# Conv accumulators in pairs, six input blocks ahead of the first gate, weight stores in ScalarE's queue: a hybrid S5/Conformer layer

## Chip, cores and metric

One core of a Trainium2 chip. The metric is the device time of one execution in microseconds: the median of three runs.

## What is computed

One decoder layer over a prompt of 2048 rows of width 1024, and beside it one step for each of 8 decoding sequences. All data is float32.

```python
h = rmsnorm(x); p = h @ w_in                      # 1024 -> 512 (S5 input u) + 512 (conv value) + 512 (conv gate)
s = s5(u)                                         # 32 groups, 64 complex states: h_t = A h_(t-1) + B u_t
a = gelu(Re(C h) + D u); s = a * sigmoid(a @ w_glu + b_glu)
z = value * sigmoid(gate)
c = swish(layernorm(causal_dwconv31(z)))          # 31 taps for each channel
x = x + rmsnorm(concat(s, c) @ w_out)
u = causal_dwconv3(rmsnorm(x) @ w_up)             # 1024 -> 2 x 2816
y = x + rmsnorm((silu(u_gate) * u_val) @ w_down)  # 2816 -> 1024
```

The last states and the last rows of both convolutions are outputs too.

## The kernel before

**Tiles and rounds.** The positions are cut into six tiles, five of 344 and one of 328 with the 8 decoding rows behind it (TILES, L24). Two tiles make a round. Activations lie with channels on partitions. Each matrix product is done with three float32r products: weights and activations are split into a high part (rounded, by ScalarE) and a low part (the rest, by VectorE), and `group` (L1105) issues high x high, high x low and low x high for each slice of 128 rows. A group of a w_in block is 24 matmuls for one tile, so a block is 48 for a round.

**Order of TensorE's work.** ORDER (L32) lists it: the input projection of rounds 0 and 1 (`mix_in`, L1954), four of the twelve blocks of round 2, then the gate and output projection of round 0 (`mix_out`, L2008, "out(0)" below), the other eight blocks, then the ConvFFN (`ffn`, L2071) of round 0, and so on. IN_ORDER (L31) gives the blocks' order: 0 to 3 make u, 4 to 7 the conv value, 8 to 11 the conv gate. `mix_out` starts with the product with w_glu, the first gate, then takes eight w_out blocks for each tile: their first four slices read sHL (the gated S5 output), their last four cHL (the split conv output).

**Weights.** `w_next` (L872) hands out blocks in the order of the list `wl`. A block's first use loads it raw (`w_load_to`, L835), splits it (`w_split_to`, L851: ScalarE writes wh, VectorE wlo) and, if it is used again, stores both parts in device memory (wd, L865 to L867). Later uses load the two parts. Each of wraw, wh and wlo has three buffers. All these transfers are issued by SyncE (SP).

**Work beside it.** Generators run beside the main order: the S5 parts (`s5_part`: products into R, a scan on VectorE in place, products into ya), the depthwise convolution (`conv`, L1677), the norms (`mid`, L1799: residual, second norm; `split_ffn`, L1813: splits its output into h for the ConvFFN). `spawn` gives each a due time; `tick` lets them emit while an estimate of each engine's clock stays within a lead of TensorE's. `after(ns)` makes a generator wait; the norms wait by NORM (L42). What is recorded so is put into the final order of each engine by a list scheduler (`Recorder.place`, L253), which works with estimated durations; on the chip each engine runs its own list in order.

**The conv.** For each of four channel blocks k and each half of a round (344 or 336 positions), 31 VectorE instructions accumulate the taps into a PSUM tile of the pool ps_cv (one bank): the first multiplies and adds the bias, the others multiply by a tap's weight and add the accumulator, the last writes the result to SBUF over the input. In round 0, block 0 and the second half of block 1 are done by ScalarE and GpSimd (`conv_pool`, L1653).

**PSUM.** Eight banks: four for matrix products (ps_mm), one for the conv (ps_cv), three for transposes and small products (ps_tr), the last counted by TRP (L682).

Of the kernel before, what the change touches and what calls it, by code (L numbers as in the profile page):

```python
# [7 lines left out]
F32 = mybir.dt.float32  # L8
# [10 lines left out]
KC = 31  # L19
# [9 lines left out]
S5_TURN = [7500, 7500, 7500]  # L29
PARTS = [4, 4, 4, 4, 6]  # L30
IN_ORDER = [4, 8, 5, 9, 0, 1, 2, 3, 6, 10, 7, 11]  # L31
ORDER = [("in", 0, 0, 12), ("in", 1, 0, 12), ("in", 2, 0, 4), ("out", 0), ("in", 2, 4, 12), ("ffn", 0, 0),  # L32
         ("out", 1), ("ffn", 0, 1), ("ffn", 1, 0), ("out", 2), ("ffn", 1, 1), ("ffn", 2, 0), ("ffn", 2, 1)]
SLOT = 2872
WARM = [8, 6, 8]
# [496 lines left out]
def kernel(  # L532
# [10 lines left out]
    def pool(name, bufs, **kw):  # L543
        return Pool(nc, ctx.enter_context(tc.tile_pool(name=name, bufs=bufs, **kw)), bufs)
# [4 lines left out]
    small = pool("small", 2)  # L549
    dram = pool("dram", 1, space=bass.MemoryType.DRAM)  # L550
    ps_mm = pool("ps_mm", NPS, space=bass.MemoryType.PSUM)
    ps_cv = pool("ps_cv", 1, space=bass.MemoryType.PSUM)
    ps_tr = pool("ps_tr", 3, space=bass.MemoryType.PSUM)


    clk = {"pe": 0.0, "act": 0.0, "dve": 0.0, "pool": 0.0}
# [31 lines left out]
    def stt(out, a, s, b, op0, op1):  # L588
        clk["dve"] += size(out) * 1.04 + 64.35
        nc.vector.scalar_tensor_tensor(out, a, s, b, op0=op0, op1=op1)  # L590
# [88 lines left out]
        def give(self, n=1):  # L679
            self.used -= n  # L680

    RAW, ROW, TRP, MSQ = Sem(2), Sem(4), Sem(3), Sem(2)  # L682
    live = [0]
    reserve = [1]

# [165 lines left out]
    def w_split_to(i):  # L851
        while w_pos[1] <= min(i, len(wl) - 1):
            n = w_pos[1]
            if n in halves:
                hl = w_shaped(n, halves.pop(n))
            else:
                raw = w_raw.pop(n)
                flat = w_tiles(n)
                hl = w_shaped(n, flat)
                with nc.first(700 if n > 1 else 0):  # L860
                    act(hl[0], raw)
                    m = hl[0].shape[1] // 2
                    for c in (slice(0, m), slice(m, 2 * m)):
                        tt(hl[1][:, c], raw[:, c], hl[0][:, c].bitcast(F32), OP.subtract)
                if n in staged:  # L865
                    for k in range(2):
                        nc.sync.dma_start(staged[n][:, k], flat[k].bitcast(F32))  # L867
            w_hl[n] = hl
            w_at[n] = max(clk.values())
            w_pos[1] += 1  # L870
# [806 lines left out]
    def conv(r):  # L1677
# [14 lines left out]
        for k in range(4):  # L1692
            yield flag("z", r, k)
            if r == 0:
                nc.sync.dma_start(c[:, k, KC - 1:], zd[:, k, 0:ntot])
            else:
                nc.sync.dma_start(c[:, k, :], zd[:, k, t0 - KC + 1:t0 + ntot])
            flags["zl", r, k] = True
            if r == 0 and k == 0:
                continue  # L1700
            yield after(3000)
            for h, t in ((h, t) for h in range(1 if r == 0 and k == 1 else 2) for t in reversed(range(KC))):
                if t == KC - 1:
                    acc = ps_cv.tile([128, 512], F32, name="acc", tag="cv")
                    a = acc[:, :hw]
                zi = c[:, k, h * hw + t:h * hw + t + hw]
                w = V2[:, k, t:t + 1]
                clk["dve"] += 65
                if t == KC - 1:
                    ts(a, zi, w, V2[:, k, KC:KC + 1], OP.mult, OP.add)  # L1710
                elif t:
                    stt(a, zi, w, a, OP.mult, OP.add)
                else:
                    stt(zi, zi, w, a, OP.mult, OP.add)
                if t % 2:
                    yield lambda: not scans[0]
            if k == 1:
                flags["half",] = True
# [521 lines left out]
```

## Time and profile before

| | |
|---|---|
| median of three runs | 2274.2 us (2268.81 to 2280.34) |
| the profiled execution | 2275.12 us |
| its span, first to last instruction | 2273.3 us |
| PE (TensorE) busy | 2198.1 us |
| DVE (VectorE) busy | 1537.4 us |
| ACT (ScalarE) busy | 865.2 us |
| mean granted clock of TensorE | 0.976 |

The engines' busy times overlap. PEclk is the share of full speed that TensorE was granted: 1.00 is 2.4 GHz, 0.50 is 1.2 GHz, and values between are a mean of the two over the stretch. In the rows, names are those of the program with buffer numbers left out: ps is a PSUM tile of a matrix product, trp one of ps_tr, acc<-c,V,acc a step of the conv, acc<-ps,FC,acc a step of the ConvFFN's short convolution, wd the stored weights. All rows name L408, the helper that emits the recorded instructions, so tiles tell them apart. A wait is put down to what came last. SPq and ACTq are DMA issues in the queues of SyncE and ScalarE.

### The profile page before, as it was taken

How to read it: one execution, taken by the hardware profiler on the slowest of the kernel's cores; microseconds unless marked ns; L12 is line 12 of the kernel's file. 1: busy time of each engine (PE TensorE's matmuls, PEld its weight loads, DVE VectorE, ACT ScalarE, POOL GpSimd, SP SyncE). 2: the span in 40 equal slices, each digit the busy share in tenths (PEclk: the TensorE clock that was granted, in tenths of full speed). 3: DMA queues.
4: the chain of work that ended last, by engine and by line, in shares of the span. 5: the costliest groups of instructions: out<-in, count | busy, mean ns of one | idle time of the engine just before them, and what ended most of it. 6: DMA issues, size and time to landing. Idle time of an engine off the chain costs nothing.

```text
span 2273.3 us, 37171 instructions
## 1 busy us (share of the span) xinstructions
PE 2198.1 (97%) x14115; PEld 2180.7 (96%) x14115; DVE 1537.4 (68%) x3554; ACT 865.2 (38%) x1661; POOL 101.9 (4%) x112
## 2 busy tenths in 40 slices
PE   8998889999999999999899999999999999999998
PEld 8998889999999999999899999999999999999998
DVE  7969966368999996745797999555447624334344
ACT  5666345245432334534434312134235322113134
POOL 1555000000000000000000000000000000000000
PEclk9998879999999999999999999999999999999999
DMA  9989857896767476588765543445685443443546
GB/s 303 276 282 274 208 162 265 272 264 216 228 217 232 165 249 210 171 313 297 226 194 171 170 137 120 156 136 188 217 292 202 165 147 119 160 147 113 191 159 216
DMA packets 278527, 467.82 MB, mean 206 GB/s; under 512 B 70176, under 2 KB 167192, under 8 KB 274709
## 3 DMA queue, kind: packets, MB, share of 16 engines
q1 hardware_dynamic: 277606, 464.08, 63.4%
q8 instruction: 112, 1.84, 0.3%
q0 software_dynamic: 352, 0.67, 0.1%
q10 hardware_dynamic: 391, 0.69, 0.1%
q14 instruction: 66, 0.54, 0.1%
HBM read 324.48 MB, written 140.37 MB: 204 GB/s over the span
## 4 chain that ended last, share of the span: by engine, by line
PE 86%; DVE 7%; DMA 4%; ACT 1%; SPq 1%; issue 1%; POOL 0%; DVEq 0%; ACTq 0%; POOLq 0%
PE ps L408 81%; PE trp L408 5%; DVE acc L408 2%; DMA wlo<-wd 2%; DVE ST L408 1%; DVE UR L408 1%; DVE mx L408 1%; DMA xb<-in_x_prompt_dram 1%; SPq L408 1%; ACT UR L408 0%; DMA ud<-us 0%; DMA UR<-ud 0%; DMA UR<-uds 0%; DVE h L408 0%; DVE w L408 0%
## 5 line engine op out<-in xcount | busy, mean ns | idle before, releaser
L408 PE MATMUL ps<-h,wh 128*128 128x346 f32 (+3 forms) x5376 | 1298.0, 324 | 16.6 <-ACT us L408 7.7
L408 PEld LDWEIGHTS ps<-h,wh 128*128 128x128 f32 x5376 | 937.8, 190 | 19.1 <-ACT us L408 7.8
L408 PE MATMUL ps<-h,wlo 128*128 128x346 f32 (+3 forms) x2688 | 867.4, 323 | 0.7 <-DMA wlo<-wd 0.7
L408 PE MATMUL ps<-f,wh 128*128 128x344 f32 (+1 forms) x2112 | 503.2, 322 | 12.0 <-ACT sq L408 8.3
L408 PEld LDWEIGHTS ps<-h,wlo 128*128 128x128 f32 x2688 | 510.2, 190 | 1.0 <-DMA wlo<-wd 0.9
L408 DVE SCALAR_TENSOR_TENSOR acc<-ps,FC,acc 128x344 f32<-128x344 f32 (+1 forms) x528 | 301.1, 570 | 248.9 <-ACT acc L408 173.3
L408 PEld LDWEIGHTS ps<-f,wh 128*128 128x128 f32 x2112 | 366.7, 190 | 12.6 <-ACT sq L408 8.5
L408 DVE SCALAR_TENSOR_TENSOR acc<-c,V,acc 128x344 f32<-128x344 f32 (+1 forms) x609 | 349.4, 574 | 10.5
L408 PE MATMUL ps<-f,wlo 128*128 128x344 f32 (+1 forms) x1056 | 339.3, 321 | 0.0
L408 ACT ACTIVATE acc<-ps,FC 128x344 f32<-128x344 f32 (+1 forms) x264 | 167.1, 633 | 396.0 <-PE ps L408 395.7
L408 PEld LDWEIGHTS ps<-f,wlo 128*128 128x128 f32 x1056 | 200.0, 189 | 0.0
L408 DVE TENSOR_TENSOR y<-y,ps 128x344 f32<-128x344 f32 (+1 forms) x192 | 97.2, 508 | 112.3 <-PE ps L408 112.0
L408 DVE TENSOR_TENSOR wlo<-wraw,wh 128x512 fp32r<-128x512 f32 (+2 forms) x212 | 122.3, 618 | 36.8 <-ACT wh L408 32.5
L408 ACT ACTIVATE f<-acc 128x344 fp32r<-128x344 f32 (+1 forms) x132 | 64.6, 489 | 201.0 <-DVE acc L408 200.7
L408 ACT ACTIVATE wh<-wraw 128x1024 fp32r<-128x1024 f32 (+2 forms) x106 | 96.6, 912 | 100.7 <-PE ps L408 90.4
L408 ACT ACTIVATE acc<-acc 128x344 f32<-128x344 f32 (+1 forms) x132 | 64.6, 489 | 159.1 <-DVE acc L408 157.5
L408 DVE TENSOR_TENSOR msq<-msq,sq 128x344 f32<-128x344 f32 (+1 forms) x84 | 43.0, 513 | 107.6 <-ACT sq L408 107.3
L408 PE MATMUL ps<-sHL,wh 128*128 128x344 f32 (+1 forms) x384 | 94.5, 329 | 2.8 <-DMA wh<-wd 2.8
L408 PE MATMUL ps<-cHL,wh 128*128 128x344 f32 (+1 forms) x384 | 93.1, 326 | 3.7 <-ACT cHL L408 3.5
L408 DVE TENSOR_TENSOR f<-acc,f 128x344 fp32r<-128x344 f32 (+1 forms) x132 | 67.5, 511 | 37.3 <-ACT f L408 36.7
L408 POOL TENSOR_TENSOR cacc<-cacc,wk 128x344 f32<-128x344 f32 x87 | 85.8, 987 | 89.4 <-ACT wk L408 84.8
L408 PEld LDWEIGHTS ps<-cHL,wh 128*128 128x128 f32 x384 | 68.0, 193 | 4.2 <-ACT cHL L408 3.8
(230 smaller groups left out, 2053.8 us busy)
## 6 DMA issues: line engine op xcount, KB each, us to landing
wh<-wd SPq DMA_DIRECT2D x156, 512.0 KB
wlo<-wd SPq DMA_DIRECT2D x156, 512.0 KB
wd<-wh SPq DMA_DIRECT2D x66, 512.0 KB
wd<-wlo SPq DMA_DIRECT2D x66, 512.0 KB
wraw<-in_w_up_dram SPq DMA_DIRECT2D x44, 512.0 KB
wh<-wd SPq DMA_DIRECT2D x64, 256.0 KB
wlo<-wd SPq DMA_DIRECT2D x64, 256.0 KB
wh<-wd SPq DMA_DIRECT2D x24, 384.0 KB
```

The source lines that it names most:

```text
L408: o.call(*[real(a) for a in o.args], **{k: real(a) for k, a in o.kw.items()})
```

## The change

Four edits in three parts. `ORDER` puts six blocks of round 2 ahead of out(0) in place of four, and six behind it in place of eight. `w_split_to` issues the stores of the split weights from ScalarE's queue in place of SyncE's. In `conv`, both halves of a channel block are accumulated tap by tap in turn, each in a bank of its own: ps_cv has two banks, and ps_tr two in place of three (TRP goes with it). Where a block has one half only (round 0, k = 1), its steps stay one behind the other.

```diff
--- before.py
+++ after.py
@@ -29,7 +29,7 @@
 S5_TURN = [7500, 7500, 7500]
 PARTS = [4, 4, 4, 4, 6]
 IN_ORDER = [4, 8, 5, 9, 0, 1, 2, 3, 6, 10, 7, 11]
-ORDER = [("in", 0, 0, 12), ("in", 1, 0, 12), ("in", 2, 0, 4), ("out", 0), ("in", 2, 4, 12), ("ffn", 0, 0),
+ORDER = [("in", 0, 0, 12), ("in", 1, 0, 12), ("in", 2, 0, 6), ("out", 0), ("in", 2, 6, 12), ("ffn", 0, 0),
          ("out", 1), ("ffn", 0, 1), ("ffn", 1, 0), ("out", 2), ("ffn", 1, 1), ("ffn", 2, 0), ("ffn", 2, 1)]
 SLOT = 2872
 WARM = [8, 6, 8]
@@ -549,8 +549,8 @@
     small = pool("small", 2)
     dram = pool("dram", 1, space=bass.MemoryType.DRAM)
     ps_mm = pool("ps_mm", NPS, space=bass.MemoryType.PSUM)
-    ps_cv = pool("ps_cv", 1, space=bass.MemoryType.PSUM)
-    ps_tr = pool("ps_tr", 3, space=bass.MemoryType.PSUM)
+    ps_cv = pool("ps_cv", 2, space=bass.MemoryType.PSUM)
+    ps_tr = pool("ps_tr", 2, space=bass.MemoryType.PSUM)
 
 
     clk = {"pe": 0.0, "act": 0.0, "dve": 0.0, "pool": 0.0}
@@ -679,7 +679,7 @@
         def give(self, n=1):
             self.used -= n
 
-    RAW, ROW, TRP, MSQ = Sem(2), Sem(4), Sem(3), Sem(2)
+    RAW, ROW, TRP, MSQ = Sem(2), Sem(4), Sem(2), Sem(2)
     live = [0]
     reserve = [1]
 
@@ -864,7 +864,7 @@
                         tt(hl[1][:, c], raw[:, c], hl[0][:, c].bitcast(F32), OP.subtract)
                 if n in staged:
                     for k in range(2):
-                        nc.sync.dma_start(staged[n][:, k], flat[k].bitcast(F32))
+                        nc.scalar.dma_start(staged[n][:, k], flat[k].bitcast(F32))
             w_hl[n] = hl
             w_at[n] = max(clk.values())
             w_pos[1] += 1
@@ -1699,20 +1699,20 @@
             if r == 0 and k == 0:
                 continue
             yield after(3000)
-            for h, t in ((h, t) for h in range(1 if r == 0 and k == 1 else 2) for t in reversed(range(KC))):
-                if t == KC - 1:
-                    acc = ps_cv.tile([128, 512], F32, name="acc", tag="cv")
-                    a = acc[:, :hw]
-                zi = c[:, k, h * hw + t:h * hw + t + hw]
+            halves_ = range(1 if r == 0 and k == 1 else 2)
+            accs = [ps_cv.tile([128, 512], F32, name="acc", tag="cv")[:, :hw] for _ in halves_]
+            for t in reversed(range(KC)):
                 w = V2[:, k, t:t + 1]
-                clk["dve"] += 65
-                if t == KC - 1:
-                    ts(a, zi, w, V2[:, k, KC:KC + 1], OP.mult, OP.add)
-                elif t:
-                    stt(a, zi, w, a, OP.mult, OP.add)
-                else:
-                    stt(zi, zi, w, a, OP.mult, OP.add)
-                if t % 2:
+                for h in halves_:
+                    zi, a = c[:, k, h * hw + t:h * hw + t + hw], accs[h]
+                    clk["dve"] += 65
+                    if t == KC - 1:
+                        ts(a, zi, w, V2[:, k, KC:KC + 1], OP.mult, OP.add)
+                    elif t:
+                        stt(a, zi, w, a, OP.mult, OP.add)
+                    else:
+                        stt(c[:, k, h * hw:h * hw + hw], zi, w, a, OP.mult, OP.add)
+                if t % 2 or len(halves_) > 1:
                     yield lambda: not scans[0]
             if k == 1:
                 flags["half",] = True
```

## Rows read from the trace of the kernel before

**Rows 1.** The page: busy time of each engine, share of the span, instructions.

```profile
PE 2198.1 (97%) x14115; PEld 2180.7 (96%) x14115; DVE 1537.4 (68%) x3554; ACT 865.2 (38%) x1661; POOL 101.9 (4%) x112
```

**Rows 2.** Table by stage: busy us of each engine, granted clock, DMA share.

```profile
28.00:110.00 82.00, 81.44 (x550) 80.00 (x548) 79.47 (x280) 52.82 (x93) 26.00 (x27) 1.00 0.97 288
...
194.00:215.00 21.00, 13.16 (x57) 12.88 (x57) 20.64 (x57) 10.20 (x27) 3.48 (x4) 0.59 1.05 300
...
248.00:310.00 62.00, 46.03 (x242) 43.77 (x242) 51.48 (x132) 21.72 (x44) 0.00 (x0) 0.70 0.63 178
...
365.00:376.00 11.00, 7.33 (x36) 6.77 (x35) 6.30 (x10) 7.34 (x12) 0.00 (x0) 0.84 0.49 160
...
395.00:412.00 17.00, 12.55 (x68) 11.66 (x67) 9.94 (x33) 4.55 (x11) 0.00 (x0) 0.83 0.99 358
...
412.00:500.00 88.00, 88.00 (x579) 87.93 (x579) 41.01 (x105) 30.73 (x62) 0.00 (x0) 0.99 0.88 254
...
500.00:1079.00 579.00, 577.61 (x3726) 575.63 (x3725) 467.72 (x1006) 240.24 (x431) 0.00 (x0) 1.00 0.70 231
...
1079.00:1092.00 13.00, 4.72 (x18) 4.46 (x17) 13.00 (x30) 7.54 (x17) 0.00 (x0) 0.61 0.77 281
```

**Rows 3.** Waits of PE from 190 to 310 us: total, times, longest.

```profile
PE trp L408 <- DVE ST L408: 9.9, 1, 9.9
...
PE ps L408 <- ACT us L408: 7.7, 1, 7.7
```

**Rows 4.** Timeline of DVE, 276 to 305 us: start, us, instruction.

```profile
297.16 0.87 DVE L408 TENSOR_TENSOR h<-xT,h 128x688 fp32r<-128x688 f32 x1
```

**Rows 5.** Waits of PE from 364 to 376 us.

```profile
PE ps L408 <- ACT cHL L408: 3.5, 1, 3.5
```

**Rows 6.** Issues of SP, 360 to 416 us, and the chain, 370 to 440.

```profile
391.72 2.92 SPq L408 DMA_DIRECT2D wd<-wh  x1
...
395.91 3.06 SPq L408 DMA_DIRECT2D wh<-wd  x1
...
399.07 8.49 DMA wlo<-wd
```

**Rows 7.** Timeline of DVE, conv steps: start, us, instruction, xcount.

```profile
146.68 7.37 DVE L408 SCALAR_TENSOR_TENSOR acc<-c,V,acc 128x344 f32<-128x344 f32 x12
...
227.30 4.28 DVE L408 SCALAR_TENSOR_TENSOR acc<-c,V,acc 128x344 f32<-128x344 f32 x7
...
639.64 0.57 DVE L408 SCALAR_TENSOR_TENSOR acc<-c,V,acc 128x344 f32<-128x344 f32 x1
...
640.12 0.57 DVE L408 SCALAR_TENSOR_TENSOR acc<-ps,FC,acc 128x344 f32<-128x344 f32 x1
...
640.61 1.19 DVE L408 SCALAR_TENSOR_TENSOR acc<-c,V,acc 128x344 f32<-128x344 f32 x2
```

**Rows 8.** Waits of PE over the whole span, transposes evicted by ScalarE.

```profile
PE trp L408 <- ACT bgt L408: 0.9, 2, 0.7
```

**Rows 9.** Behind out(0): PE, DVE timelines; last line: PE waits, 1075 to 1095.

```profile
436.61 0.48 PE L408 MATMUL ps<-h,wh 128*128 128x344 f32 x2
...
478.29 0.35 DVE L408 SCALAR_TENSOR_TENSOR st<-st 86x4 f32<-86x4 f32 x2
...
488.55 3.99 DVE L408 SCALAR_TENSOR_TENSOR mx<-mx,V,sqs 128x344 f32<-128x344 f32 x8 [1.98 <-ACT sqs L408]
...
494.45 2.44 DVE L408 TENSOR_TENSOR h<-mx,h 128x688 fp32r<-128x688 f32 x3
...
PE ps L408 <- ACT sq L408: 8.3, 1, 8.3
```

**Rows 10.** Stores to wd on SP (ns min/median/max); SP waits for wlo.

```profile
L408 SPq DMA_DIRECT2D wd<-wh x106: 319/320/4170, 19.2 to 1109.0; - x106
...
L408 SPq DMA_DIRECT2D wd<-wlo x106: 319/320/3592, 23.3 to 1110.0; - x106
...
SPq L408 <- DVE wlo L408: 70.2, 79, 3.6
```

## The prediction

> **What bounds the kernel now.** I read the page's engine line first, then a table by stage, then the waits of TensorE inside the stages that lose time, and last single rows of the engines behind those waits. The engine line [rows 1] says that TensorE is the bound: PE is busy 2198.1 of 2273.3 us, so at most 75 us can be won from idle time, plus what is lost while the granted clock is low. The stage table [rows 2] shows where both sit. From 500 to 1079 us PE is busy 577.61 of 579 us at clock 1.00: nothing done to VectorE or to the queues pays there. The losses of the first 420 us are, ahead of all, in 194 to 215 (13.16 busy at 0.59), 248 to 310 (46.03 of 62 at 0.70), 365 to 376 (7.33 of 11 at 0.84) and 395 to 412 (12.55 of 17 at 0.83). Taking clock times span as full-speed time, 194 to 215 and 248 to 310 give up some 13 and 29 us.
>
> In these two stages VectorE is the bound, not TensorE: DVE is busy 20.64 of 21 us in the first. TensorE's two longest waits there [rows 3] are 9.9 us for the scan of the S5 part (ST) and 7.7 us for a ScalarE eviction that waits for a VectorE gate. VectorE begins the first low part of h for round three at 297.16 [rows 4], and mix_in(2) has no complete product before it. From 365 to 376 the wait is for cHL, the split conv output [rows 5], 3.5 us. From 395 to 412 it is a load of staged weights [rows 6].
>
> **The change, part by part.** *Conv accumulators in turn.* A conv half is 31 VectorE instructions, each reading the accumulator that the one before wrote. One that directly follows its own half starts 0.61 us after it: twelve in 7.37 us, seven in 4.28 us [rows 7]. With another instruction between, starts are 0.48 us apart (639.64, 640.12, 640.61) [rows 7]. So each direct successor costs 0.125 us too much. Between the first and the last of these runs, 146 to 232 us, twelve runs and their neighbours hold 72 direct successors; after that the conv already alternates with the scan. 72 x 0.125 = 9.0 us of VectorE, all ahead of the 297 us at which it releases TensorE, in a stretch where it hardly idles. I take all 9.0 as gain. Bounds: 0, if another wait ends last; 42 (13 + 29), if both holes close. Round one's half at k=1 stays single; the halves of rounds two and three lie beside a full TensorE (500 to 1079 us) [rows 2] and I cost them at nothing: that cover is large, and the change only relieves VectorE there.
>
> The Trainium skill (VectorE: DVE Perf Modes, The DRAIN you can't avoid) says that the next VectorE instruction doesn't start until the pipeline is empty, and that how instructions are chained changes nothing. By that rule the two spacings would be equal and this part worth 0, the sum -1.4; rows 7 show two spacings.
>
> *One transpose bank fewer* (ps_tr 3 to 2). A transpose waits for the eviction two before it, not three. TensorE's waits for evicted transposes are small now (0.9 us in two waits for bgt [rows 8]). Bounds 0 and, if each of those two waits became one eviction longer (the row's longest, 0.7), 1.4 more; no gain is possible, since nothing gets more room. I take 0.5.
>
> *Six blocks before the gate.* Two w_in blocks move from behind out(0) to ahead of it. A block is 48 matmuls at 577.61/3726 = 0.155 us [rows 2], 7.4 us; two are 14.9 us. They bring four weight loads, four us evictions and four ud stores ahead of the gate's weights on SP; those ran beside a full PE and a two-thirds idle ScalarE (412 to 500: 30.73 of 88 us) [rows 2]. The gain: cHL, now 3.5 us late, is covered. The stage 365 to 376 loses 3.67 us idle and (1 - 0.84) x 11 = 1.76 of clock: 5.4 us. Bounds 0 and 5.4; I take 5.4, since 14.9 is four times the wait.
>
> What is late next: the six blocks left behind out(0) cover 44.6 us where eight covered 59.5. They hide the chain mid, split_ffn for tile 1. It runs from out(0)'s end, 436.61, to the last low half of h, 494.45 + 2.44 = 496.89 [rows 9]: 60.3 us, as long as today's cover. After the change TensorE asks for tile 0 at 481.2 and, one group of 24 matmuls (3.7 us) later, for tile 1 at 484.9, on the old time axis. The last reciprocal root was done at 478.64, its broadcast used at 488.55 [rows 9]; I read these 9.9 us as pacing, because 5000 ns of wait is written into NORM and VectorE idles. If it keeps its length, the first pieces of h come at about 493.3, 8.4 us late. If TensorE's idleness lets the transposes through at once, scaling starts near 482, and h's first pieces come at 487: 2 late. With half a clock after the wait, as from 1079 to 1092 (13 us, 4.72 busy, clock 0.61, after an 8.3 us wait) [rows 2, 9], the bounds are 0 and 12; I take 4.
>
> *Stores from ScalarE.* 212 stores leave SP. An issue takes 0.32 us at the median, 4.17 at most [rows 10], so ScalarE gets some 68 us of issue against 1400 us idle. The new waits: a wlo store waits on ScalarE for VectorE's subtract (70.2 us in 79 waits on SP now [rows 10]); queued behind it are PSUM evictions, h splits and ConvFFN's Silu. TensorE waits for those, but has four PSUM tiles of 3.7 us. At the very start TensorE's first products need ScalarE's splits of h, and the stores of the first two blocks, four at 0.32 us, land between them: 1.3 us. I take 1.5. Bounds: 0, and one longest wlo issue, 3.59 us, for each of the twelve w_in blocks, where DVE is busy 79.47 of 82 us and ACT 52.82 [rows 2]: 43 us of ScalarE, of which 29 are idle anyway, so 14. A gain here: staged loads no longer queue behind stores. In 377 to 407 SP issues stores of 2.92 us, then a load that takes 3.06, and the chain stands 8.49 us on the load issued at 399.07 [rows 6]. That stage loses 17 - 12.55 = 4.45 idle and some 2.1 of clock: bounds 0 and 6.6. DMA share there is 0.99, so most must remain: I take 2.
>
> The Trainium skill (DMA: Bandwidth & Descriptors, Issuing engines are not separate DMA queues) has the transfers of all issuing engines on the same 16 DMA engines, so that another issuer saves only sequencer time; by that rule these 2 us fall to 0 and the sum to -8.4.
>
> Sum: -9.0 + 0.5 - 5.4 + 4 + 1.5 - 2 = -10.4 us. It is made against the profiled execution, 2275.1 us, 0.9 above the median of 2274.2. From the median: 2263.8, so 2264.
>
> **The rivals.** *VectorE's saving doesn't reach TensorE.* Its chain could be set by loads or by evictions, or the instruction order could put the same waits elsewhere. For: the 7.7 us wait goes through ScalarE. Against: DVE is busy 20.64 of 21. Without the 9.0: 2273. The rule of the Trainium skill quoted above (VectorE: DVE Perf Modes, The DRAIN you can't avoid) would give this time too. *The cover is missed.* Pacing stays whole and the clock halves: +12 in place of +4, 2272; for it speaks the 1079 row, against it that VectorE is only half busy from 412 to 500. *Every hole closes:* 9.0 + 5.4 + 6.6, nothing lost behind out(0), and the clock of the 194 stage kept (half of its 8 us of clock loss, 4): 25 less, 2250. *ScalarE is held by its stores, and it is slower.* Place: 28 to 110 us and the gate, where VectorE and ScalarE feed each other. Each held wlo store delays evictions that VectorE's gates need, and VectorE has no slack. It decides once a block's stores hold ScalarE over 2.4 us (29 idle / 12). Price: 14 in place of 1.5, VectorE's 9.0 eaten, and 2 more at the gate, where two pairs come: -10.4 + 12.5 + 9 + 2 = +13, 2287. That the change doesn't do what it says would be seen as 0.61 us spacing in the conv; it is part of the first rival.
>
> **How the numbers follow.** A measurement can tell about 0.5% from no change, 11.4 us: below 2262.8 is faster, above 2285.6 slower. Forecast 0.52, its own range 2254 to 2274 and so a little under half of it below 2262.8 (0.25 faster, 0.27 the same); every hole closes 0.17 (faster); saving lost 0.07 and cover missed 0.07 (the same); ScalarE held 0.17 (slower). Faster 0.42, the same 0.41, slower 0.17. The range goes from 2247, below the case of closed holes, to 2285, which leaves out most of the slow case.
>
> **What would show it.** In the changed profile: conv starts 0.48 to 0.5 us apart throughout; h for round three before 290; no wait for cHL; PE from 248 to 310 at least 9 us fuller; the stores in ScalarE's queue at a third of a us; a wait for h or mx of 2 to 8 us at the head of ffn(0,0). Wrong it is if ScalarE's evictions show waits for VectorE's wlo, if the 194 and 248 holes keep their size, or if the holes only move behind out(0).

## The result, and the profile after

The changed kernel is slower: 2289.1 us (median of four executions, 2288.3 to 2293.8) against 2271.5 for the kernel before beside it, ratio 1.0075 with a 95% interval of 1.0053 to 1.0097. A second measurement gave 1.0076 (1.0054 to 1.0097). I had predicted 2264 and a range up to 2285. The profiled execution took 2288.8 us, its span is 2287.0.

The page's engine line after the change, which answers to [rows 1]:

```profile
PE 2196.7 (96%) x14115; PEld 2172.3 (95%) x14115; DVE 1509.4 (66%) x3554; ACT 866.9 (38%) x1662; POOL 109.9 (5%) x112
```

TensorE's work is the same, but it stands idle for 2287.0 - 2196.7 = 90.3 us where it stood 75.2. VectorE has 28 us less to do and GpSimd 8 us more. The table by stage (columns as in [rows 2]; the first line is the kernel before from 120 to 146 us, all others are the changed kernel):

```profile
120.00:146.00 26.00, 26.00 (x175) 26.00 (x174) 15.45 (x25) 15.31 (x30) 8.97 (x10) 0.93 0.92 284
...
28.00:110.00 82.00, 81.90 (x558) 80.73 (x557) 78.07 (x285) 48.43 (x85) 18.66 (x21) 1.00 0.97 297
120.00:146.00 26.00, 19.30 (x90) 18.16 (x89) 9.81 (x16) 15.71 (x28) 12.87 (x15) 0.70 0.82 305
194.00:215.00 21.00, 16.96 (x97) 16.96 (x98) 15.89 (x42) 5.88 (x11) 4.78 (x4) 0.80 0.75 219
248.00:310.00 62.00, 44.95 (x283) 42.16 (x284) 53.56 (x158) 22.94 (x47) 0.00 (x0) 0.89 0.73 192
365.00:376.00 11.00, 9.89 (x58) 9.02 (x58) 10.23 (x18) 8.81 (x18) 0.00 (x0) 1.00 0.63 201
395.00:412.00 17.00, 12.41 (x70) 11.41 (x68) 3.99 (x12) 3.63 (x7) 0.00 (x0) 0.90 1.04 398
412.00:500.00 88.00, 79.36 (x491) 78.57 (x492) 41.78 (x119) 26.02 (x54) 0.00 (x0) 0.92 0.94 272
500.00:1079.00 579.00, 575.67 (x3702) 572.30 (x3700) 457.45 (x999) 239.48 (x430) 0.00 (x0) 1.00 0.70 226
```

The stages that I wanted filled are not: 248 to 310 has 44.95 busy (46.03 before), 395 to 412 has 12.41 (12.55). Two stages that were full are not any more: from 120 to 146 TensorE is busy 19.30 of 26 us at 0.70 (26.00 at 0.93 before), and from 412 to 500 it is busy 79.36 of 88 where it was never idle [rows 2]. The second is in part a shift: with two blocks more ahead of it out(0) ends at 457 us, where it ended at 436, and takes its waits for weights along. Only 365 to 376, the wait for cHL, is better (9.89 for 7.33).

The waits of TensorE from 100 to 300 us in the changed kernel (total, times, longest), which answer to [rows 3]:

```profile
PE trp L408 <- ACT ST L408: 11.7, 1, 11.7
PE ps L408 <- ACT vt L408: 9.1, 3, 8.1
PE trp L408 <- issue: 3.9, 1, 3.9
```

and those from 397 to 445 us:

```profile
PE ps L408 <- DMA wh<-wd: 5.3, 2, 4.3
PE ps L408 <- DMA wlo<-wd: 2.8, 2, 2.0
```

The waits for ST (9.9) and us (7.7) of [rows 3] have their like in ST (11.7) and vt (8.1), vt being an evicted tile of the conv value; the staged weights of out(0) now come 4.3 us late at the worst.

The conv does what the diff says. A row of VectorE's timeline after the change:

```profile
163.66 17.49 DVE L408 SCALAR_TENSOR_TENSOR acc<-c,V,acc 128x344 f32<-128x344 f32 x36
```

and the page's group of conv steps after the change (busy, mean ns, idle before):

```profile
L408 DVE SCALAR_TENSOR_TENSOR acc<-c,V,acc 128x344 f32<-128x344 f32 (+1 forms) x609 | 314.7, 573 | 1.0
```

36 steps in 17.49 us are 0.48 us apart, where twelve direct successors took 7.37 [rows 7]. The same group of the kernel before reads:

```profile
L408 DVE SCALAR_TENSOR_TENSOR acc<-c,V,acc 128x344 f32<-128x344 f32 (+1 forms) x609 | 349.4, 574 | 10.5
```

So VectorE's saving is real (44 us over the whole kernel with the idle time; 9 of it in the stretch of my count, 146 to 232 us), and the question is where TensorE lost it.

### The profile page after: what moved, and what is told of

Read it like the earlier page. It is cut to its first block, busy times and chain, and to the rows that moved or that the text cites. A ratio compares the mean times of both kernels' runs of the same rounds, so it can differ in the third digit from the quotient of the medians.

```text
span 2287.0 us, 37153 instructions
## 1 busy us (share of the span) xinstructions
PE 2196.7 (96%) x14115; PEld 2172.3 (95%) x14115; DVE 1509.4 (66%) x3554; ACT 866.9 (38%) x1662; POOL 109.9 (5%) x112
## 4 chain that ended last, share of the span: by engine, by line
PE 82%; DMA 6%; DVE 6%; ACT 3%; issue 1%; POOL 1%; SPq 1%; DVEq 0%; ACTq 0%; POOLq 0%
PE ps L408 78%; PE trp L408 4%; DMA wlo<-wd 2%; DVE ST L408 1%; DVE UR L408 1%; DVE acc L408 1%; ACT UR L408 1%; SPq L408 1%; POOL cacc L408 1%; DMA xa<-in_x_prompt_dram 1%; DVE mx L408 1%; DMA wraw<-in_w_out_dram 1%; DMA UR<-Cd 1%; ACT wk L408 1%; DVE wlo L408 0%
## 5 line engine op out<-in xcount | busy, mean ns | idle before, releaser
L408 DVE SCALAR_TENSOR_TENSOR acc<-c,V,acc 128x344 f32<-128x344 f32 (+1 forms) x609 | 314.7, 573 | 1.0
L408 ACT ACTIVATE wh<-wraw 128x1024 fp32r<-128x1024 f32 (+2 forms) x106 | 96.7, 913 | 104.8 <-PE ps L408 97.1
L408 POOL TENSOR_TENSOR cacc<-cacc,wk 128x344 f32<-128x344 f32 x87 | 93.3, 1073 | 103.9 <-ACT wk L408 88.9
L408 PEld LDWEIGHTS ps<-sHL,wh 128*128 128x128 f32 x384 | 68.7, 195 | 10.7 <-issue 4.5
```

Source lines behind the costliest of these rows:

```text
L408: o.call(*[real(a) for a in o.args], **{k: real(a) for k, a in o.kw.items()})
```

## The experiments

All ratios are to the kernel before, timed beside each run. I call the conv with its banks A, the six blocks B, the stores from ScalarE C.

**The parts alone, and the banks alone.** The first three are the change's hunks one by one. The fourth is A without its loop:

```diff
-    ps_cv = pool("ps_cv", 1, space=bass.MemoryType.PSUM)
-    ps_tr = pool("ps_tr", 3, space=bass.MemoryType.PSUM)
+    ps_cv = pool("ps_cv", 2, space=bass.MemoryType.PSUM)
+    ps_tr = pool("ps_tr", 2, space=bass.MemoryType.PSUM)
-    RAW, ROW, TRP, MSQ = Sem(2), Sem(4), Sem(3), Sem(2)
+    RAW, ROW, TRP, MSQ = Sem(2), Sem(4), Sem(2), Sem(2)
```

> The conv part alone (pairs, two conv banks, two transpose banks), eight of 12 blocks behind out(0) and stores on SP as before. Theory 1 (the order is what costs: out(0) waits for its staged weights because two more blocks stand ahead of it): this part is worth its price or less, 2 to 9 us under the kernel before (ratio 0.996 to 0.999), and out(0) waits no longer than before, under 8 us lost from 395 to 445 us. Theory 2 (the stores on ScalarE are what costs: stores land later, so the staged loads that wait for them do): the same 2 to 9 us under. Theory 3 (the change to the conv makes another static order of all engines, with its own waits): 5 to 15 us over (ratio 1.002 to 1.007), with a wait of 10 us or more between 240 and 300 us for the scan of the S5 part, as the changed kernel has at 275 to 285.

> Six w_in blocks of round three ahead of the first gate, nothing else changed. Theory 1 (the order costs): 8 to 16 us over the kernel before (ratio 1.0035 to 1.007), with TensorE waiting 6 us or more for wlo and wh from DRAM in the 60 us of out(0), where the kernel before waits about 4. Theory 2 (the stores on ScalarE cost): 0 to 5 us under, the wait for cHL gone and out(0) no worse than before. Theory 3 (the conv's new order costs): the same as theory 2.

> The stores of the split weights from ScalarE, nothing else changed. Theory 2 (these stores cost): 8 to 16 us over the kernel before (ratio 1.0035 to 1.007), TensorE losing 3 us or more in each of 10 to 28 us and 110 to 140 us more than before, and out(0) waiting 6 us or more for staged weights. Theory 1 and theory 3: within 3 us of the kernel before (ratio 0.9987 to 1.0013), with out(0)'s waits for staged weights as long as before or shorter.

> Only the banks: two conv banks and two transpose banks, the conv still one half after the other. My prediction put one transpose bank fewer at 0.5 us, with 1.4 as its bound: ratio 1.000 to 1.001. Theories 1 and 2 say the same. Theory 3 in the form that the lost transpose bank, not the pairs, makes the new waits: 5 us or more over (ratio above 1.002), with waits of TensorE for evicted transposes of over 4 us in all.

Measured: A 1.0039 (1.0024 to 1.0054), B 1.0010 (0.9999 to 1.0021), C 0.9997 (0.9988 to 1.0007), the banks alone 1.0025 (1.0014 to 1.0037). Theories 1 and 2 fall: alone, neither the six blocks nor the stores cost anything clear of noise. A alone costs 8.9 us (0.0039 x 2271); by the middle values more than half of it comes with the banks, but their intervals overlap. Theory 3 has A's time and not its place: no wait for the scan of 10 us is there, TensorE's longest from 240 to 300 us is 4.2. The banks alone also bring the spacing: their group of conv steps has 318.9 us busy and 1.2 idle. With a second bank the list scheduler interleaves the two halves by itself, without the new loop.

**What of A costs.** Two transpose banks with one conv bank; A with three transpose banks and three product banks; A without the charge for a direct successor; the kernel before without that charge. The edits:

```diff
-    ps_tr = pool("ps_tr", 3, space=bass.MemoryType.PSUM)
+    ps_tr = pool("ps_tr", 2, space=bass.MemoryType.PSUM)
...
-NPS = 4
+NPS = 3
...
-                    clk["dve"] += 65
```

> The kernel before with two transpose banks in place of three, still one conv bank (one bank is left unused). The two bank edits together cost 5.0 us, the conv part in whole 10.4. Theory 3a (the lost transpose bank is what costs): 4 to 11 us over the kernel before (ratio 1.0018 to 1.0048). Theory 3b (the second conv bank, by which the conv runs ahead of the scan of the S5 part, is what costs): within 2 us (0.999 to 1.001). Theory 3c (any new static order costs some us): 3 us or more over, with waits at other places than the runs with two conv banks have.

> The conv part in pairs with two conv banks and three transpose banks; the bank is taken from the product accumulators instead, three for four. Theory 3a: 3 to 9 us under the kernel before in the first 400 us, as the transposes have their third bank; what three product banks cost shows as PE idle from 500 to 1079 us, where the kernel before loses 1.4 us, and is to be read apart. Theory 3b: first product with the gated tile (a) and first product with cHL no earlier than in the run of the conv part alone, and the time 8 us or more over. Theory 3c: as 3b.

> The conv part as in the change, but the planner's charge of 65 ns of VectorE for each conv instruction taken out: that charge stands for the wait of a direct successor, which pairs no longer have. Theory 3d (the old charge makes the planner bring VectorE's other work too late or too early): 4 to 10 us under the run of the conv part alone, at or under the kernel before (ratio 0.998 to 1.0005). Theories 3a to 3c: no gain over the conv part alone beyond 3 us (ratio 1.0025 to 1.006).

> The kernel before with the same charge taken out: same instructions, same banks, one conv half after the other, only the static order of the engines differs. Theory 3c (the order of before is a favourable one, and a new order costs some us whatever made it): 3 us or more over (ratio above 1.0013). Theories 3a, 3b and 3d: within 3 us, since no resource changes.

Measured: 1.0013 (1.0001 to 1.0025), 1.0035 (1.0021 to 1.0049), 1.0037 (1.0015 to 1.0059), 0.9997 (0.9985 to 1.0010). The lost transpose bank costs some 3 us (0.2 to 5.7), a third of A. Giving it back at the expense of a product bank gains nothing; no rows are read from these two. 3d falls: the charge is not it. 3c in its general form falls too: the last run has another static order and costs nothing. That it is A's own order that costs the rest is what is left over; no run shows it by itself.

**The parts in pairs.** Hunks of the change, two by two, and the whole change once more.

> The change without its third part: the conv part and the six blocks ahead, stores on SP. By addition of what the parts cost alone (10.4 and 1.0): 11 us over, ratio 1.005. Theory R (the changed kernel's loss of some 8 us in out(0) needs the stores on ScalarE, which send SP on to loads that then fill the DMA engines): 1.003 to 1.006 here and out(0) loses under 4 us. Theory S (it comes of the conv part and the order together, as the DMA engines are short of bytes after the stall at 190 us and out(0) comes no later): 1.006 to 1.009 here, out(0) loses 6 us or more.

> The changed kernel once more, for a second profile and more times beside these. By the first measurement 17 us over, ratio 1.0075. By addition of the parts alone 11 us, ratio 1.005. Theory P says in addition that every execution has a long GpSimd add or none: the profile shows one of 8 us or more between 170 and 200 us where the time is 2288 or more, and none where it is under 2280.

> The change without its second part: conv part and stores on ScalarE, four blocks ahead of the gate. The parts alone cost 10.4 and 0. Theory V (the conv part and the stores clash, whatever the blocks): 15 us or more over, ratio above 1.0065. Otherwise, if the clash needs all three parts or each order is its own case: 5 to 12 us over, ratio 1.002 to 1.0055.

> The change without its first part: six blocks ahead of the gate and stores on ScalarE, conv as before. The parts alone cost 1.0 and 0. Theory V: within 4 us, ratio 0.998 to 1.002. If the six blocks and the stores clash, so that out(0) finds the DMA engines full: 8 us or more over, ratio above 1.0035, with 6 us or more lost in out(0).

This was the surprise:

| parts | ratio (95%) | sum of the parts alone |
|---|---|---|
| A + B | 0.9973 (0.9956 to 0.9990) | 1.0049 |
| A + C | 1.0093 (1.0080 to 1.0106) | 1.0036 |
| B + C | 0.9982 (0.9972 to 0.9992) | 1.0007 |
| A + B + C | 1.0076 (1.0054 to 1.0097) | 1.0046 |

**A and B together are faster than before** (6 us), B and C too (4 us; the two are not told apart), and C, which alone costs nothing, adds 0.0103 to them, 23 us. Theories R, S and V were put for sums that do not exist: V has the sign of the clash right (A with C), but no theory expected A + B under 1. The long GpSimd add that theory P speaks of (below) is in the second profile of the changed kernel too, an execution of 2286.6 us.

Why B helps A can be read. Columns as in [rows 2], 320 to 345 us of A alone:

```profile
320.00:345.00 25.00, 18.36 (x104) 16.94 (x103) 16.03 (x25) 18.54 (x27) 0.00 (x0) 0.73 0.57 167
```

and the stretch ahead of the same gate in A + B, with two blocks more in it:

```profile
300.00:355.00 55.00, 55.00 (x374) 54.34 (x373) 29.86 (x63) 32.28 (x53) 0.00 (x0) 1.00 0.81 212
```

With A alone TensorE comes to its first gate early and finds its operands not ready: 6.6 us idle, and (1 - 0.73) x 25 = 6.8 of clock. With the blocks TensorE has no idle time there.

**Order or issuing engine.** What does C do to A + B? These two runs keep the order of one kernel on TensorE, VectorE and GpSimd, instruction for instruction, and change only the engine that issues the stores:

```diff
-                        nc.sync.dma_start(staged[n][:, k], flat[k].bitcast(F32))
+                        nc.sync.dma_start(staged[n][:, k], flat[k].bitcast(F32), by=nc.scalar)
```

for the order of A + B, and `nc.scalar.dma_start(..., by=nc.sync)` for the order of A + B + C; `by` replaces the engine after the order is made.

> The static order of the run with two parts (conv part and six blocks; 2265.7 us), instruction for instruction on TensorE, VectorE and GpSimd, but the stores of the split weights are issued by ScalarE, at their place in that order. Theory T (the issuing itself costs nothing; what costs is the order that the planner makes once the stores count as ScalarE's): 2262 to 2270 us, ratio 0.996 to 0.999. Theory U (ScalarE is held by its stores, as each waits for VectorE's low half or for an earlier transfer, and evictions stand behind it): 2278 us or more, ratio above 1.003.

> The static order of the changed kernel (2289 us), instruction for instruction on TensorE, VectorE and GpSimd, but the stores are issued by SP as before the change. Theory T: 2283 to 2292 us, ratio 1.005 to 1.009. Theory U: 2274 us or less, ratio under 1.002.

Measured: order of two, stores by ScalarE, 0.9997 (0.9981 to 1.0012); order of three, stores by SP, 1.0052 (1.0038 to 1.0066).

| | stores by SP | stores by ScalarE |
|---|---|---|
| order of A + B | 0.9973 | 0.9997 |
| order of A + B + C | 1.0052 | 1.0076 |

Down a column, the order costs 0.0079, 18 us; along a row, the issuing costs 0.0024, some 5.5 us, twice (each with an error of about 0.0025, as large as itself; the two together are clear of it). Theory T holds in the main and U in part. **By these values three quarters of the 23 us are the new static order, a quarter is ScalarE's issuing.**

In the order of two the issuing can be seen at the start. ScalarE's timeline, 17 to 28 us, in the order of two with stores by ScalarE:

```profile
18.11 0.76 ACT L408 ACTIVATE h<-xn 128x688 fp32r<-128x688 f32 x1
23.40 0.33 ACTq L408 DMA_DIRECT2D wd<-wlo  x1
23.83 1.06 ACT L408 ACTIVATE xn<-xb 88x1024 f32<-88x1024 f32 x1 [4.96 <-DMA rows<-in_g_post_mix_dram]
```

and with the same order, stores by SP:

```profile
18.66 0.76 ACT L408 ACTIVATE h<-xn 128x688 fp32r<-128x688 f32 x1
19.72 1.06 ACT L408 ACTIVATE xn<-xb 88x1024 f32<-88x1024 f32 x1 [0.30 <-DMA xb<-in_x_prompt_dram]
```

The first of the two again: its chain of waits, 18 to 30 us, and TensorE's product behind:

```profile
9.04 14.33 DMA rows<-in_g_post_mix_dram
...
25.70 0.66 PE L408 MATMUL ps<-h,wh 128*128 128x344 f32 x1 [4.07 <-ACT h L408]
```

ScalarE stands from 18.87 to 23.40 in front of its store, until a load lands that SP issued at 9.04 (9.04 + 14.33 = 23.37), and which has nothing to do with the store's data. TensorE's product behind it comes 4.07 us late. I had put 1.3 us there for four issues. What couples the two is a semaphore. In the trace the program's 1214 transfers from SP and ScalarE tell of their landing by eight semaphores, taken in turn. This store and that load, the eighth transfer ahead of it, have the same one, and the store waits for it before its issue. (The list scheduler reckons with that: the eight lanes in `place`, L274.)

The changed kernel has no such stand at the start. ScalarE's holds ahead of its stores lie elsewhere; two of them, each with the product of TensorE that waits behind it for wh:

```profile
121.70 1.06 ACT L408 ACTIVATE wh<-wraw 128x1024 fp32r<-128x1024 f32 x1 [1.95 <-DMA wh<-wd]
122.81 0.90 PE L408 MATMUL ps<-h,wh 128*128 128x344 f32 x4 [1.53 <-ACT wh L408]
...
401.44 0.55 ACT L408 ACTIVATE mx<-ps,V 128x344 f32<-128x344 f32 x1 [3.39 <-DMA xr<-xTd]
403.33 0.67 PE L408 MATMUL ps<-sHL,wh 128*128 128x344 f32 x2 [2.42 <-ACT wh L408]
```

Both holds end with the landing of a load that SP issued. They are not the whole account: with the same order and the stores on SP TensorE waits 1.9 us at the second place too.

**What the order costs.** One profiled execution each, read from TensorE's timeline: the first product with w_glu (its input is tile a; 14.9 us taken off where two blocks more stand ahead), the length of out(0) from there to its last product, and from there to the last w_up product (14.9 us put on). Executions of one kernel differ by more than many of these differences: the kernel before took 2265.5 to 2280.3 us in the first measurement, and the one shown here, 2275.1, lies 3.6 over the median; A + B took 2260.8 to 2274.2, and 2263.6 here.

| | first gate | out(0) | rest |
|---|---|---|---|
| before | 339.7 | 96.7 | 1770.9 |
| A | 335.2 | 100.3 | 1776.3 |
| A + B | 325.3 | 97.6 | 1773.1 |
| order of two, by ScalarE | 329.1 | 99.7 | 1772.7 |
| order of three, by SP | 336.0 | 101.6 | 1777.6 |
| A + B + C | 337.1 | 104.9 | 1779.1 |
| A + B + C, second profile | 335.1 | 104.9 | 1778.8 |

In these executions A + B reaches the gate 14 us earlier than before. That is more than the 9 us of my sum, as the holes close with their clock; A + B from 194 to 215 and from 248 to 310 us:

```profile
194.00:215.00 21.00, 20.62 (x140) 20.28 (x138) 21.00 (x48) 14.29 (x31) 13.87 (x15) 1.00 1.07 229
248.00:310.00 62.00, 59.94 (x366) 58.87 (x365) 44.85 (x126) 19.21 (x34) 0.00 (x0) 0.89 0.77 228
```

The order of three gives some 11 of these back, whoever issues the stores. Against the kernel before, then, the changed one is not late at the gate; it loses 8 us in out(0) and 8 behind it. VectorE's longest wait from 100 to 300 us in the changed kernel:

```profile
DVE h L408 <- PE ps L408: 15.2, 1, 15.2
```

and in A + B:

```profile
DVE gt L408 <- ACT gt L408: 9.7, 3, 7.2
```

In the changed kernel VectorE stands 15.2 us, from 125 to 141, at a low half of h whose tile TensorE still reads, while TensorE itself is late (the 120 to 146 stage). The conv behind it begins at 155.3, in A + B at 143.9. And GpSimd: durations of its conv adds (ns, min/median/max), in the kernel before:

```profile
L408 POOL TENSOR_TENSOR cacc<-cacc,wk x87: 911/932/1615, 71.8 to 228.7; 128x344 f32<-128x344 f32 x87
```

and in the changed one:

```profile
L408 POOL TENSOR_TENSOR cacc<-cacc,wk x87: 909/931/9692, 84.1 to 242.2; 128x344 f32<-128x344 f32 x87
```

One add takes 9.7 us. It stands in the chain of waits of the changed kernel (180 to 200 us), with ScalarE's product and the eviction vt behind it, for which TensorE waits 8.1 us:

```profile
186.34 9.70 POOL cacc L408
...
197.06 0.58 ACT wk L408
197.64 0.35 ACT vt L408
```

While it lasts VectorE runs the products that build CA, a matrix of the S5 part, one behind the other. The three runs with A and C, and the order of three with SP's stores, all have this add and the wait of 13 to 16 us; A + B and the order of two have neither.

The add does not need C. The banks alone and A without its charge have a longer one; the adds of both, and TensorE's wait in the banks alone, 100 to 300 us:

```profile
L408 POOL TENSOR_TENSOR cacc<-cacc,wk x87: 906/930/12628, 77.7 to 235.4; 128x344 f32<-128x344 f32 x87
L408 POOL TENSOR_TENSOR cacc<-cacc,wk x87: 909/932/12732, 78.3 to 235.2; 128x344 f32<-128x344 f32 x87
PE ps L408 <- ACT vt L408: 19.2, 2, 17.8
```

Their times fall in two groups each: the banks alone nine times 2272.7 to 2277.7 us and three times 2282.7 to 2285.4, A without its charge seven times 2273.2 to 2278.0 and five times 2288.2 to 2292.6. Both profiles (2283.4 and 2288.2 us) are of the upper group. So part of what A costs may be this add, in some executions of one and the same order and not in others. That the lower group lacks it is not shown, as none of it was profiled; A's own profile, at 2279.6 us, has no add over 1.9.

**The long add, by itself.** Two kernels with the whole computation left out, as the expectations say. The first lets GpSimd's adds and VectorE's products enter together; in the second each add waits for a product of ScalarE, as in the conv, and comes after VectorE has begun:

```diff
+            nc.scalar.activation(wk[q % 2], z[:, 600:944], AF.Copy, scale=2.0)
+            nc.gpsimd.tensor_tensor(cacc, cacc, wk[q % 2], op=OP.add)
...
+            nc.vector.tensor_tensor(w[q % 4], a, z[:, 256:512], op=OP.mult)
```

> The whole computation is left out; in its place stand the kernel's own kinds of instruction, in six stretches that both engines enter together: eight GpSimd adds of 128x344 alone; 36 VectorE products of 128x256 with both inputs in SBUF (as in the building of the S5 matrices) alone; both together; the adds beside 24 conv steps on two PSUM accumulators in turn; beside 24 on one accumulator; beside six groups of six such products with one conv step between groups. Theory P (a GpSimd add that reads SBUF is locked out as long as VectorE runs such products back to back, and a conv step, with one SBUF input, lets it in): 0.93 us an add alone, in the third stretch one add of 8 us or more that ends when the 36 products do (36 x 0.33 = 12 us), in the two conv stretches 0.9 to 1.2 us an add, in the last about one add per group. Theory Q (the long add of the changed kernel has another cause): adds of under 2 us in all stretches.

> The whole computation is left out; GpSimd's adds stand here as in the conv, each behind a product that ScalarE makes for it, and they begin some 2 us after VectorE's run. Six stretches: eight adds alone; beside 36 products with both inputs in SBUF; beside 24 conv steps on two accumulators; on one; beside six groups of six products and one conv step; beside six groups of six products and two conv steps. Theory P2 (an add that arrives while VectorE's products run back to back gets in only when they end or a conv step comes): in the second stretch one add of 6 to 11 us, in the grouped stretches adds of 2 to 3 us each, in the conv stretches 1.2 us at most. Theory Q2 (GpSimd gets in between any two instructions, as when its adds ran without gaps): all adds under 1.5 us and VectorE's products slower instead.

The first, VectorE's timeline, the 36 products alone and with the adds:

```profile
14.65 12.16 DVE L95 TENSOR_TENSOR w<-z 128x256 f32<-128x256 f32 x36 [8.87 <-ACT z L86]
27.38 17.87 DVE L95 TENSOR_TENSOR w<-z 128x256 f32<-128x256 f32 x36 [0.57 <-ACT z L86]
```

The second, VectorE's timeline, the products beside the adds:

```profile
17.27 12.16 DVE L95 TENSOR_TENSOR w<-z 128x256 f32<-128x256 f32 x36 [11.45 <-ACT z L86]
```

GpSimd's timeline in the second, the eight adds beside them:

```profile
19.94 17.18 POOL L110 TENSOR_TENSOR cacc<-cacc,wk 128x344 f32<-128x344 f32 x8 [3.27 <-ACT wk L109]
```

and the adds' durations over all stretches of the second (ns, min/median/max):

```profile
L110 POOL TENSOR_TENSOR cacc<-cacc,wk x48: 907/911/10265, 8.8 to 95.0; 128x344 f32<-128x344 f32 x48
```

In the first run P was wrong: no add stood, the engines took turns. Beside the adds, in the first, eight products of VectorE and the eight adds of GpSimd:

```profile
27.72 8.48 DVE L95 TENSOR_TENSOR w<-z 128x256 f32<-128x256 f32 x8
27.49 8.43 POOL L90 TENSOR_TENSOR cacc<-cacc,z 128x344 f32<-128x344 f32 x8 [13.44 <-ACT z L86]
```

Both go at 1.05 us from one to the next, in place of 0.34 for a product alone and 0.98 for an add alone; 8 x 0.71 = 5.7 us is what VectorE lost (17.87 - 12.16). In the second it is as P2 said for the second stretch: VectorE takes its 12.16 us as if alone, and the longest add takes 10.27 us. The products end at 17.27 + 12.16 = 29.43; the long add is the first, begun at 19.94, and ends 0.8 us after them. P2 was wrong for the grouped stretches: once GpSimd had got in at a conv step the engines took turns again, and eight adds took 10.05 and 8.20 us. Beside conv steps every stretch of eight took 7.8 us, as alone. The 24 conv steps themselves, on two accumulators in turn and on one, in the second kernel:

```profile
37.63 11.70 DVE L100 SCALAR_TENSOR_TENSOR acc<-z,acc 128x344 f32<-128x344 f32 x24 [8.20 <-ACT z L85]
49.66 14.76 DVE L100 SCALAR_TENSOR_TENSOR acc<-z,acc 128x344 f32<-128x344 f32 x24 [0.33 <-ACT z L85]
```

**Taking the long add out of the changed kernel.** First by giving GpSimd one instruction in six of CA's building, which makes the planner write a new order:

```diff
-            tt(CA[0][:, :, t], w1, w2, OP.subtract, "any")
+            tt(CA[0][:, :, t], w1, w2, OP.subtract, "pool")
```

> The changed kernel with one of the six instructions of each of the eight steps that build CA given to GpSimd, so that VectorE's run of 48 products is cut into runs of five. Theory P (in the changed kernel the gain of VectorE ends in a GpSimd add that is locked out for 9.7 us, and behind it ScalarE and TensorE wait): the longest add of the conv's GpSimd part under 3 us, TensorE's wait for vt gone or under 4 us (8.1 in the changed kernel), and 5 to 12 us under the changed kernel, 2276 to 2284. Theory Q (the wait comes from the order in ScalarE's queue, not from the lock): the same wait of 7 us or more, and within 3 us of the changed kernel.

Measured: 1.0070 (1.0051 to 1.0090). The longest add is 2.3 us and the wait for vt 1.6, but TensorE now waits 13.6 us for tile a ahead of the gate:

```profile
351.02 0.94 PE L408 MATMUL ps<-a,wh 128*128 128x344 f32 x2 [13.63 <-ACT a L408]
```

Within 3 us of the changed kernel, as Q said, though by another wait. Then with the order kept: after the planner is done, 20 conv steps move up in VectorE's list alone (i0: behind the last wlo; g: the next gate; i1: the conv's first step):

```diff
+        lines["dve"] = d[:i0] + d[i1:i1 + 10] + d[i0:g] + d[i1 + 10:i1 + 20] + d[g:i1] + d[i1 + 20:]
```

> The changed kernel with 20 conv steps moved up in VectorE's queue, the order of every other engine kept: ten go ahead of the low half of h at which VectorE stands 13 to 15 us from 124 us on, ten ahead of the next gate, where it stands 4.5 to 4.9 us. Their rows of the convolution are there at about 135 us, so that VectorE can win some 4.8 us at the first place and 4.9 at the second. Theory W (VectorE, late from there on, is what TensorE waits for at the scan's ST, 9 to 12 us, near 275 to 285 us): that wait falls by 4 us or more and the run is 4 to 10 us under the changed kernel (ratio to before 1.003 to 1.006). Theory X (what sets the time ahead of the gate is not VectorE's lateness but the long GpSimd add and the weights from DRAM): within 3 us of the changed kernel (1.0065 to 1.009), the wait for ST shorter but others longer.

Measured: 2283.1 us, 1.0043 (1.0027 to 1.0059), 6 us under the changed kernel. Its waits of TensorE, 100 to 300 us:

```profile
PE trp L408 <- ACT ST L408: 12.6, 1, 12.6
...
PE ps L408 <- ACT vt L408: 1.1, 2, 0.7
```

and the durations of its GpSimd adds:

```profile
L408 POOL TENSOR_TENSOR cacc<-cacc,wk x87: 906/931/1687, 84.0 to 234.0; 128x344 f32<-128x344 f32 x87
```

The time is what theory W forecast, but not by its way: the wait for ST is as long as ever, and what went is the long add and the wait for vt behind it (9.1 to 1.1). The conv's rows landed only at 139, so VectorE stood 13.6 us for them instead of for h and won nothing there. So some 6 of the 18 us of the order went with the long add in one run that moved 20 conv steps, and none in the other, which made a new order: that the 6 are the add's own is likely, not shown. The rest (out(0), and the part behind it) I did not take apart by a run.

## Why the prediction was wrong

**The step that failed is the sum itself.** It priced each part on the order of the kernel before and added up. But the orders of all engines are written anew by the list scheduler for each edit, and the parts do not add: alone they come to +10 us (my sum for them was -10.4), A + B to -6, all three to +17. The two runs on fixed orders show what the sum had no term for: 18 us of the 23 between A + B and all three are another order.

- *Conv in turn, -9.0.* The spacing was right, 0.48 us, and the second small kernel shows it too: 14.76 - 11.70 = 3.06 us for 24 steps, 0.13 each. The Trainium skill's rule as the prediction quotes it (VectorE: DVE Perf Modes, The DRAIN you can't avoid) would have this part at nothing, and these rows are against that; the same paragraph lets a next instruction that is not held start earlier. "I take all 9.0 as gain" failed: with A alone TensorE loses it at a gate that it reaches too early, in out(0) and behind it; with B it is won; with C VectorE stands 15 us at a tile and GpSimd's add 9.7 us. My rival "VectorE's saving doesn't reach TensorE" named "the same waits elsewhere", but priced them as the old waits, so that it could not be slower than before. Its bound of 42 comes from busy time times clock, not from the span as its sentence says; nothing else hangs on it.
- *One transpose bank fewer, 0.5.* Measured 3.0 us (0.2 to 5.7): over my bound of 1.4 by its middle, though the interval holds both. Counting two waits of the old order was no bound for the new one.
- *Six blocks, -5.4 and +4.* The wait for cHL is gone, as forecast. Alone it measures +2.3 us (-0.2 to 4.8), sum -1.4: just outside. What is late next was right in size: from out(0)'s last product to the second gate the changed kernel takes 533.7 us, 2.8 more than before with the two blocks taken off, where I took 4. What I missed is that its worth depends on A: on top of A it is worth 1.0039 - 0.9973 = 0.0066, 15 us, as it covers holes which A opens.
- *Stores from ScalarE, -0.5.* Alone right: 0.7 us under (-2.7 to +1.6). The loads gained nothing at 395 to 412 us (12.41 busy, 12.55 before), as the rule quoted from the Trainium skill (DMA: Bandwidth & Descriptors, Issuing engines are not separate DMA queues) would have it. On a given order they cost 5.5 us, more than my 1.5 and within its bounds. The rival "ScalarE is held by its stores" came nearest to the time (2287), and that was luck: it charged ScalarE with all of the loss, where the order has three quarters. An issue takes 0.33 us, 1.4 at most, and the holds that can be seen in front of TensorE end with another engine's transfer. For wlo 64 stores of the changed kernel stand 0.3 to 1.2 us each, but all except two of them after 480 us, beside a TensorE that is busy 575.67 of 579 us. The store issues of the changed kernel on ACTq, ScalarE's sequencer (ns, min/median/max, and where they lie):

```profile
L408 ACTq DMA_DIRECT2D wd<-wh x106: 326/326/1434, 23.2 to 1117.5; - x106
L408 ACTq DMA_DIRECT2D wd<-wlo x106: 326/380/1362, 27.6 to 1118.7; - x106
```

- *What would show it.* Conv spacing (but for round one's single half), no wait for cHL and the issue times came. The h of round three, forecast before 290, begins at 291.9, in the second profile at 289.5 (297.2 before [rows 4]); 248 to 310 was not fuller; no wait for h or mx of 2 us or more came at the head of ffn(0,0). Of the signs named for wrong, "if the 194 and 248 holes keep their size" came for 248 to 310 (44.95 busy for 46.03), while 194 to 215 went from 13.16 to 16.96; and holes came behind the first gate, in out(0).

The version to keep is A + B: 2265.7 us, 0.9973 of before, or B + C, 0.9982, which it is not told apart from.

## What to carry to other kernels

Where a scheduler writes every engine's order from estimates, an edit is a new order first and a local saving second: price a change of several parts by its pairs, not by a sum, and give the range room for it on both sides. To tell an order's cost from an instruction's, keep the order and change only the engine, or move a few instructions in one engine's list. And a saving on a busy engine counts only as far as nothing else on the way to the bound becomes late by the new order: here it was, among others, one GpSimd add that stood 9.7 us behind VectorE's products.

## What the chip showed that I had not expected

GpSimd's adds and VectorE's products with two SBUF inputs hold each other up, and not evenly. An add that came 2.7 us into a run of 36 products stood until the run was over: 10.3 us for one of 0.91, and VectorE lost nothing. Where the first add came 0.1 us behind the first product, the two took turns: 1.05 us from one to the next on both engines, and 17.87 us for products that take 12.16. What decides between standing and taking turns is not shown. Conv steps, with one input in PSUM, do not disturb GpSimd (eight adds in 7.8 us). The Trainium skill (SBUF — State Buffer, Who interferes with whom) says that such a VectorE instruction contends with a GpSimd instruction that reads SBUF, and that the order of issue decides who blocks. The trace agrees on which instructions; on how long it goes further, as the add stood not for one product but for the rest of the run, some 28.

A store in ScalarE's queue stood 4.5 us until an unrelated load of SP's queue had landed, and ScalarE's work behind it with it. By the trace both use one of eight landing semaphores, which the program's transfers take in turn: the store was the eighth transfer behind the load.
